# The low part of k laid out twice, so that both score products use 128 rows

## Chip, cores and metric

The kernel runs on one core of one Trainium2 chip. The metric is the device time of one execution, in microseconds (us); the time before is 1805.77 us, the median of three runs (1802.51 to 1806.38). PE is the matrix engine, PEld its weight loads, DVE VectorE, ACT ScalarE, POOL GpSimd, SP the engine that issues most transfers.

## The reference

Two layers of a transformer trunk over 256 latent tokens and 256 context tokens of width 1024. In each layer three attention branches and a Fourier branch read one projection; their gated sum is projected out and normalised, and an expert-choice layer of 16 experts follows. In the second layer only the latent tokens go on. The attention has four query heads of 64 features and two key heads, each shared by two query heads:

```python
def gqa_softmax(q, k, v, bias=None, sink=None):
    s = jnp.einsum("bqhgd,bkhd->bhgqk", q, k).astype(jnp.float32) * HEAD_DIM ** -0.5
    if bias is not None:
        s = s + bias
    ...
        p = jax.nn.softmax(s, axis=-1)
    return jnp.einsum("bhgqk,bkhd->bqhgd", p.astype(v.dtype), v)
```

The branches differ in what stands around it: branch a normalises and rotates q and k, branch c has a window and a sink, branch d a bias by relative position.

## The kernel before

Everything is float32, but the wide products run on operands of type fp32r, which the kernel splits itself: a value is hi + lo, and a product is taken as hi by hi, hi by lo and lo by hi. In the scores the split lies along the contraction. A head has 64 features, so a column of q holds 128 rows, hi above lo (lo above hi for the second key head). The tile of q, `qT`, has a block of 128 tokens' columns for each query head. The tile of k, `kT`, has three blocks of 512 tokens: hi over hi for each of the two key heads, and one block with the lo of key head 0 in rows 0 to 63 and that of key head 1 in rows 64 to 127. Two products make a score: `qT` by the hi block on all 128 rows, which gives hi by hi and lo by hi (line 642), and hi of q by lo of k on the 64 rows where both lie (line 643).

`post_vec` makes the parts in token order for one tile of 128 tokens (the copy of hi twice on ACT, line 595; lo on DVE, line 597), `post_tr` transposes them on PE (q in line 615, k in line 619) and moves them out of the bank with ACT (line 616) and with DVE (the cast of line 620). `scores` then makes the scores of one unit: either 128 latent tokens and one key head with 512 columns for two heads, or 128 context tokens with 256 columns for four heads. The scores lie in one tile of two banks, `ps`; DVE takes the maximum (line 676), ACT the exponential (line 681). One unit later the probabilities are transposed (lines 702 and 712), and after that multiplied by v (lines 724 and 733). Layer 0 has 18 units (three branches, four latent and two context each), layer 1 has 12.

This work isn't a stage of its own. `post_fill` and `attn_fill` put pieces of it into a queue, and the loops over the projection (line 531) and over the gates of the previous branches take a piece for each of their steps. A step of the gates has 24 products of line 771 and six of line 782, with weights that ACT and DVE split (lines 422 and 424) after a transfer; most steps have a modulation product too (line 217). On PE, the products of the gates and of the projection keep their order among themselves; the attention's pieces are placed between them, on PE, DVE and ACT, by a scheduler when the program is built. The order of SP's transfers and of POOL's work is that of the program text. Behind the attention come the output projection, the routing, and the experts, whose weights (1 MB a piece) go in turn into every large tile that the rest leaves free, the tile of k among them.

Two pools matter for the change: the tile of k is the only one with its tag `k8`, and the parts `o` share the tag `p` with the probabilities, whose tile is 128 by 1024.

Of the kernel before, what the change touches and what calls it, by code (L numbers as in the profile page):

```python
# [9 lines left out]
F32 = mybir.dt.float32  # L10
F32R = mybir.dt.float32r
# [75 lines left out]
def trunk(ctx: ExitStack, tc: tile.TileContext, x, c, ctx_in, c_ctx, w_mod, b_mod, w_in, qk_gain,  # L87
# [52 lines left out]
    def load_consts(l):  # L140
        """The mixers' tables, which give their place to weights once a layer's attention is done."""
        mix_cst.append(big([128, N_MIX], "cst"))
        nc.sync.dma_start(mix_cst[-1], consts[:, 0:N_MIX])
        if l == 0:
            nc.sync.dma_start(route_cst, consts[:, N_MIX:N_CONST])
# [10 lines left out]
    def ones():  # L156
        # the last column of the triangle
        return const("tri")[:, 127:128].to_broadcast([128, 128])
# [51 lines left out]
    def mod_mm(l, ch, group):  # L210
        """Partial products of one chunk, in rows 2q and 2q + 1 of each quadrant (q the chunk's place in its four)."""
        q = ch % 4
        p = ps_t()
        for r in range(2):
            for g in range(4):
                kt = 4 * r + g
                T.matmul(p[g * 32:g * 32 + 32, :], c_st[:, kt, 6 - 2 * q:38 - 2 * q], RAW["mod", l, ch, r][:, g, :],  # L217
                         start=r == 0, stop=r == 1)
        if ch == group[0]:
            mrows[l, group] = t2([128, 512])  # L220
            V.tensor_copy(mrows[l, group], p)
        else:
            m = mrows[l, group]
            V.tensor_tensor(m, m, p, op=OP.add)

    def mod_acc(l, ch, group):
        """As mod_mm, but the chunks of a group add up in a bank of their own."""
# [15 lines left out]
    def mod_tr(l, group):  # L243
        """Sums of up to four chunks, feature-major."""
# [14 lines left out]
    def mod_first(kp):  # L259
        """Shift and scale of two feature tiles, the first layer's."""  # L260
# [32 lines left out]
    def affine(l, half):  # L293
        """u = z * A + B, feature-major: the modulation, with the norm's own gain and bias folded in."""
# [64 lines left out]
    def ex_raw(l, e, kind, q):  # L359
        w = {"g": w_gate, "u": w_up, "d": w_down}[kind]  # L360

        if e == NE - 1 and kind == "d":
            # the last expert's share of the output comes by columns
            def go(t):
                nc.sync.dma_start(t, w[l, e, :, q * 256:q * 256 + 256].rearrange("(k p) n -> p k n", p=128))
            return (("ex", l, e, kind, q), [128, 8, 256], go)
# [12 lines left out]
    def ex_w(l, e, kind, k, c, n):  # L379
        """Rows k * 128.. and columns c..c + n of an expert's matrix."""  # L380
# [24 lines left out]
    def inorder(*engines):  # L405
        """What the block puts on these engines issues after the previous such block's work."""
# [10 lines left out]
    def split(key, src, alloc, eng=V):  # L417
        """hi + lo parts, each exact in the product's 12-bit significand."""
# [37 lines left out]
    def layer(l):  # L456
# [7 lines left out]
        def ut_alloc():  # L464
            if last:
                # a tile per stream: the context's go after the projections
# [33 lines left out]
        def bias_table():  # L500
            """Per-row relative-position bias, 8x, flipped into token order."""
# [43 lines left out]
        def post_alloc(m):  # L545
            qk[m] = (big([128, 4, 512], "q8", F32R), big([128, 3, 512], "k8", F32R))
            vv[m] = pool.tile([128, 4, 128], F32, name="v", tag="v", bufs=1)

        def rope(src, t, nh):
            """Rotates src [128, nh, 64] in place."""  # L550
# [11 lines left out]
        def post_norm(m, t):  # L562
            """Values aside; the norm's factors."""
# [15 lines left out]
        def post_vec(m, t):  # L579
            """norm and rotation of one token tile, split."""  # L580
# [9 lines left out]
            if lat and m != "d":  # L590
                rope(src, t, nh)
            o = b4([128, 14, 64], "p", F32R)
            ok, oq = o[:, 0:6], None
            kv_ = src[:, nq:nh]
            A.activation(ok[:, 0:4].rearrange("p (k u) d -> p k u d", u=2),
                         kv_.unsqueeze(2).to_broadcast([128, 2, 2, 64]), AF.Copy)
            V.tensor_tensor(ok[:, 4:6], kv_, ok[:, 0:4].rearrange("p (k u) d -> p k u d", u=2)[:, :, 0].bitcast(F32),
                            op=OP.subtract)
            if nq:
                oq = o[:, 6:14].rearrange("p (h s) d -> p h s d", s=2)  # L600
# [6 lines left out]
        def post_tr(m, t):  # L607
            """q blocks [hi | lo] ([lo | hi] for the second kv head), k blocks [hi | hi] x 2, [lo0 | lo1]."""
# [8 lines left out]
            p = ps_t([128, 3, 128])  # L617
            for b in range(3):
                T.transpose(p[:, b], ok[:, 2 * b:2 * b + 2].rearrange("p s d -> p (s d)").bitcast(F32), ident)
            V.tensor_copy(kT[:, :, ts], p)  # L620

# [6 lines left out]
        def br_out(m, src, kv, ts):  # L628
            """src [128, kv, tokens] to the branch, split."""
# [4 lines left out]
        def scores(m, u):  # L634
# [3 lines left out]
            def qk_mm(dst, h, t, k0, k1):  # L638
                kv = h // 2
                r = slice(64 * kv, 64 * kv + 64)  # L640
                ts = slice(t * 128, t * 128 + 128)
                T.matmul(dst, qT[:, h, ts], kT[:, kv, k0:k1], start=True, stop=False)  # L642
                T.matmul(dst, qT[r, h, ts], kT[r, 2, k0:k1], start=False, stop=True)  # L643
# [181 lines left out]
        def residual(dst, z, key):  # L825
            """alpha times the norm's output, from its normalised rows."""
# [6 lines left out]
        def y0_mm(kt):  # L833
            """Left half of the output: one merged feature tile's share, all tokens."""
# [45 lines left out]
        NS = NT // 2  # L880

        def route_weights():
            """The norm and the modulation folded into the router: logits = rstd * (h.wA - mean * sum(wA)) + B.w"""
# [15 lines left out]
        def turned(t, hf):  # L899
            """Half of the features of a token tile, feature-major."""  # L900
# [7 lines left out]
        def route_half(t, hf):  # L908
            """Router products of one half of the features of a token tile."""
# [4 lines left out]
            for k in range(4):  # L914
                # rows 0..15 of a quadrant sum its share; rows 16..31 are not used
# [20 lines left out]
        def route(t):  # L936
            """Router probabilities of one token tile; its rows normalised."""
# [14 lines left out]
        def rows(t):  # L952
            """Normalises a token tile."""
# [6 lines left out]
        def choose():  # L960
            """Slot number (1..CAP, 0 for none) of each token with each expert of its stream."""
# [34 lines left out]
        def gather(gr, s, pr):  # L996
            """Rows of the tokens that two experts chose, turned feature-major and modulated."""
# [25 lines left out]
        def gather_one(s, e):  # L1023
            """As gather, for one expert of the first group."""
# [21 lines left out]
        def scat_mat(gr):  # L1046
# [7 lines left out]
            else:  # L1054
                # the rows bring their weights along: a matrix of ones
# [96 lines left out]
        def scat_hl(s, dh):  # L1152
            """The last group's without its last expert, split."""
# [13 lines left out]
        # The last expert: partial sums over the features in row blocks (c, stream, slot), columns a quarter at  # L1167
        # a time, scattered by a matrix of ones that adds the parts up.
# [26 lines left out]
        def scat_start(t):  # L1195
            """The latents' banks begin with the rows so far."""
# [65 lines left out]
        def end_stats(s):  # L1262
            """Of both token tiles of a stream."""
# [37 lines left out]
        # ================= order of work =================  # L1301
# [379 lines left out]
    # emission: loads run LEAD tiles ahead of their use  # L1681
# [67 lines left out]
```

## Time and profile before

| | us |
|---|---|
| median of three runs | 1805.77 |
| lowest, highest | 1802.51, 1806.38 |
| span of the profiled execution | 1799.7 |
| PE busy in it | 1575.4 (88%) |
| DVE busy | 694.8 (39%) |
| ACT busy | 432.3 (24%) |

The profile is of one execution; the span runs from its first instruction to its last, and what lies around it isn't in it, so it is shorter than the runs' times. Its own time as a run would measure it isn't listed, so the span stands beside the median. Busy shares are means over the whole span. PE's durations are modelled at their ends and overlap, so a step of PE is read as the time from one instruction's start to the next one's.

### The profile page before, as it was taken

The numbers are of one execution on the slowest core, as the hardware profiler recorded it, in microseconds if no ns is written. First come the engines' busy times: TensorE is split into PE (matmuls) and PEld (weight loads), VectorE is DVE, ScalarE is ACT, GpSimd is POOL, SyncE is SP. The second block draws the span as 40 slices with busy tenths as digits, with TensorE's granted clock in tenths as the row PEclk, the third lists the DMA queues.
The fourth block names the chain that finished last, engine by engine and source line by source line (L and its number), as shares of the span: only waits on it lengthen the run. The fifth ranks groups of instructions, "written<-read, shape, count | busy, mean of one in ns | idle before, by whom it ended". The sixth has DMA issues, their size and how long they took to land.

```text
span 1799.7 us, 22915 instructions
## 1 busy us (share of the span) xinstructions
PE 1575.4 (88%) x9291; PEld 892.1 (50%) x9291; DVE 694.8 (39%) x1378; ACT 432.3 (24%) x929; POOL 129.7 (7%) x176
## 2 busy tenths in 40 slices
PE   7999999999989989899998899999978666667666
PEld 4767777768864333323332578888832211112112
DVE  3454453554452332222222585747543111102114
ACT  2343433343231110201200354544321001001000
POOL 1200112111110000000000320111100000000000
PEclk9999999999989999999999999999989889888888
DMA  9444344444559999999999664646889999999996
GB/s 310 164 149 157 119 167 107 164 140 165 216 208 365 374 408 409 409 409 409 409 409 403 234 240 169 216 111 236 327 317 409 409 409 409 409 409 409 409 409 245
DMA packets 194120, 533.04 MB, mean 296 GB/s; under 512 B 9520, under 2 KB 61088, under 8 KB 194016
## 3 DMA queue, kind: packets, MB, share of 16 engines
q1 hardware_dynamic: 192016, 527.49, 76.9%
q0 software_dynamic: 1856, 4.02, 1.3%
q8 instruction: 73, 1.20, 0.3%
q14 instruction: 31, 0.25, 0.0%
q10 hardware_dynamic: 144, 0.07, 0.0%
HBM read 530.50 MB, written 1.05 MB: 295 GB/s over the span
## 4 chain that ended last, share of the span: by engine, by line
PE 67%; DMA 15%; issue 10%; DVE 5%; ACT 2%; POOL 1%; SPq 0%; ACTq 0%; DVEq 0%; POOLq 0%
PE mm L771 14%; PE mm L1088 12%; PE mm L531 7%; DMA w<-in_w_up_dram 6%; PE mm L1109 5%; DMA raw<-in_w_up_dram 4%; PE mm L782 3%; PE pt L217 2%; PE mm L1122 2%; PE mm L851 2%; PE ps L1005 2%; DMA w<-in_w_down_dram 2%; PE ps L643 2%; PE pt L724 1%; PE ps L642 1%
## 5 line engine op out<-in xcount | busy, mean ns | idle before, releaser
L771 PE MATMUL mm<-w,b 128*128 128x512 f32 (+1 forms) x1536 | 292.6, 342 | 0.3 <-DVE b L424 0.3
L771 PEld LDWEIGHTS mm<-w,b 128*128 128x128 f32 x1536 | 236.8, 189 | 47.7 <-issue 18.6
L1077 ACT ACTIVATE t<-mm 128x512 f32<-128x512 f32 (+1 forms) x32 | 19.0, 594 | 663.2 <-PE mm L1122 352.1
L1078 DVE SCALAR_TENSOR_TENSOR t<-t,mm 128x512 f32<-128x512 f32 (+1 forms) x32 | 21.9, 684 | 358.6 <-ACT t L1077 358.5
L424 DVE TENSOR_TENSOR b<-raw,b 128x1024 fp32r<-128x1024 f32 (+1 forms) x95 | 112.7, 1189 | 122.7 <-ACT b L422 119.7
L531 PE MATMUL mm<-b,w 128*128 128x512 f32 (+1 forms) x720 | 148.9, 360 | 5.2 <-ACT b L422 3.6
L531 PEld LDWEIGHTS mm<-b,w 128*128 128x128 f32 x720 | 115.9, 192 | 30.7 <-ACT b L422 4.0
L422 ACT ACTIVATE b<-raw 128x1024 fp32r<-128x1024 f32 (+1 forms) x96 | 97.9, 1021 | 128.9 <-PE mm L771 97.5
L1095 DVE TENSOR_TENSOR k<-mm,b 32x512 f32<-32x512 f32 (+1 forms) x96 | 53.1, 553 | 187.5 <-PE mm L1109 84.6
L1088 PE MATMUL mm<-w,b 128*64 128x512 f32 x480 | 116.9, 596 | 2.1 <-DMA w<-in_w_gate_dram 1.2
L1122 PE MATMUL mm<-w,b 128*32 128x512 f32 x416 | 82.5, 665 | 26.9 <-DMA w<-in_w_up_dram 22.3
L800 POOL TENSOR_TENSOR b<-b,t 128x256 f32<-128x256 f32 x72 | 56.4, 798 | 521.6 <-DVE t L794 502.4
L1122 PE MATMUL mm<-raw,b 128*32 128x512 f32 x256 | 55.4, 733 | 30.8 <-DMA raw<-in_w_up_dram 16.1
L782 PE MATMUL mm<-w,wbs 128*128 128x512 f32 (+1 forms) x384 | 78.4, 339 | 0.1
L1088 PEld LDWEIGHTS mm<-w,b 128*64 128x64 f32 x480 | 37.9, 137 | 70.3 <-issue 63.9
L1088 PE MATMUL mm<-raw,b 128*64 128x512 f32 x280 | 70.9, 594 | 0.7 <-DMA raw<-in_w_gate_dram 0.7
L782 PEld LDWEIGHTS mm<-w,wbs 128*128 128x128 f32 x384 | 61.2, 188 | 8.8 <-ACT w L631 0.3
L1109 PE MATMUL mm<-w,t 128*64 128x512 f32 x240 | 58.4, 612 | 2.9 <-ACT t L1104 2.9
L1122 PEld LDWEIGHTS mm<-w,b 128*32 128x32 f32 x416 | 16.3, 116 | 86.8 <-DMA w<-in_w_up_dram 41.4
L681 ACT ACTIVATE p<-ps,st 128x512 f32<-128x512 f32 (+1 forms) x72 | 43.6, 613 | 55.3 <-DVE st L679 55.3
L1146 PE MATMUL ps<-k,wbs 128*128 128x512 f32 x72 | 39.7, 671 | 4.7 <-DVE k L1095 3.7
L1122 PEld LDWEIGHTS mm<-raw,b 128*32 128x32 f32 x256 | 9.8, 118 | 65.8 <-DMA raw<-in_w_up_dram 28.7
(373 smaller groups left out, 2232.6 us busy)
## 6 DMA issues: line engine op xcount, KB each, us to landing
w<-in_w_up_dram SPq DMA_DIRECT2D x64, 1024.0 KB, 18.1
w<-in_w_down_dram SPq DMA_DIRECT2D x59, 1024.0 KB, 16.6
raw<-in_w_mod_dram SPq DMA_DIRECT2D x48, 1024.0 KB, 5.2
w<-in_w_gate_dram SPq DMA_DIRECT2D x48, 1024.0 KB, 18.3
raw<-in_w_in_dram SPq DMA_DIRECT2D x46, 1024.0 KB, 6.3
raw<-in_w_down_dram SPq DMA_DIRECT2D x35, 1024.0 KB, 16.1
raw<-in_w_up_dram SPq DMA_DIRECT2D x34, 1024.0 KB, 15.3
raw<-in_w_gate_dram SPq DMA_DIRECT2D x33, 1024.0 KB, 15.3
```

Of the source, the lines that this page charges most:

```text
L422: A.activation(hi, src, AF.Copy)
L424: eng.tensor_tensor(lo, src, hi.bitcast(F32), op=OP.subtract)
L531: T.matmul(p, uu(kt, t * 128, t * 128 + 128), ww[:, kt % 2, a:n], start=kt == 0 and i == 0, stop=kt == 7 and i == 2)
L681: A.activation(P[:, hh, a:b], s[:, hh, a:b], AF.Exp, scale=0.125, bias=nm[:, n:n + 1], accum_out=rs[:, n:n + 1])
L771: T.matmul(p, ww[:, kt], uu(kt, 0, NTOK), start=n == 0, stop=n == 23)
L782: T.matmul(p, ww[:, k, o:o + 128], br[i][:, j, k], start=n == 0, stop=n == 5)
L800: G.tensor_tensor(m, m, e[:, c], op=OP.add)
L1088: T.matmul(p[fh * 64:fh * 64 + 64], xs[kt // 4][:, kt % 4, e % 4], ex_w(l, e, kind, kt, fh * 512, 512), start=kt == 0, stop=kt == 7)
L1095: V.tensor_tensor(dst, pd[q], g, op=OP.mult)
L1109: T.matmul(pd[dh * 64:dh * 64 + 64], hT[:, q, fh * 64:fh * 64 + 64], ex_w(l, e, "d", f, dh * 512, 512), start=f == 0, stop=f == 7)
L1122: T.matmul(p[r:r + 32], xs[kt // 4][:, kt % 4, e % 4], ex_w(l, e, kind, kt, fh * 512, 512), start=kt == 0, stop=kt == 7)
L1146: T.matmul(p[:, dh], loc["sm", gr][:, s, t], loc["y", gr][s][:, dh * 512:dh * 512 + 512], start=True, stop=True)
```

## The change

The tile of k gets four blocks in place of three: hi over hi for both key heads, then lo over lo for both. The second product so reads the whole column of q, 128 rows, and adds hi by lo and also lo by lo. In the diff the lines that only lose a comment are left out.

```diff
-            qk[m] = (big([128, 4, 512], "q8", F32R), big([128, 3, 512], "k8", F32R))
+            qk[m] = (big([128, 4, 512], "q8", F32R), big([128, 4, 512], "k8", F32R))
...
-            o = b4([128, 14, 64], "p", F32R)
-            ok, oq = o[:, 0:6], None
+            o = b4([128, 16, 64], "p", F32R)
+            ok, oq = o[:, 0:8].rearrange("p (i k u) d -> p i k u d", i=2, u=2), None
             kv_ = src[:, nq:nh]
-            A.activation(ok[:, 0:4].rearrange("p (k u) d -> p k u d", u=2),
-                         kv_.unsqueeze(2).to_broadcast([128, 2, 2, 64]), AF.Copy)
-            V.tensor_tensor(ok[:, 4:6], kv_, ok[:, 0:4].rearrange("p (k u) d -> p k u d", u=2)[:, :, 0].bitcast(F32),
-                            op=OP.subtract)
+            kv2 = kv_.unsqueeze(2).to_broadcast([128, 2, 2, 64])
+            A.activation(ok[:, 0], kv2, AF.Copy)
+            V.tensor_tensor(ok[:, 1], kv2, ok[:, 0].bitcast(F32), op=OP.subtract)
             if nq:
-                oq = o[:, 6:14].rearrange("p (h s) d -> p h s d", s=2)
+                oq = o[:, 8:16].rearrange("p (h s) d -> p h s d", s=2)
...
-            p = ps_t([128, 3, 128])
-            for b in range(3):
-                T.transpose(p[:, b], ok[:, 2 * b:2 * b + 2].rearrange("p s d -> p (s d)").bitcast(F32), ident)
+            p = ps_t([128, 4, 128])
+            for b in range(4):
+                T.transpose(p[:, b], ok[:, b // 2, b % 2].rearrange("p s d -> p (s d)").bitcast(F32), ident)
             V.tensor_copy(kT[:, :, ts], p)
...
-                r = slice(64 * kv, 64 * kv + 64)
                 ts = slice(t * 128, t * 128 + 128)
-                T.matmul(dst, qT[:, h, ts], kT[:, kv, k0:k1], start=True, stop=False)
-                T.matmul(dst, qT[r, h, ts], kT[r, 2, k0:k1], start=False, stop=True)
+                for i in range(2):
+                    T.matmul(dst, qT[:, h, ts], kT[:, 2 * i + kv, k0:k1], start=i == 0, stop=i == 1)
```

The change also moves instructions, since the scheduler places the attention's pieces anew. On SP and POOL nothing moves. On PE, at the first scores of layer 0's first branch (the row names the line, the tile written and those read, and the output's shape; in the kernel after the change, lines from 599 on are numbered one lower, from 644 on two lower, the copy on ACT is line 596, and both score products stand in line 641), the order before is:

```order
L615 MATMUL pt<-idsel,p 128x128 x4
L619 MATMUL pt<-idsel,p 128x128 x3
L771 MATMUL mm<-w_146,b_854 128x512
L771 MATMUL mm<-w_146,b_855 128x512
L217 MATMUL pt<-raw,c_st 32x512
L642 MATMUL ps<-k_688,q_687 128x512
L643 MATMUL ps<-k_688,q_687 128x512
L642 MATMUL ps<-k_688,q_687 128x512
L643 MATMUL ps<-k_688,q_687 128x512
L217 MATMUL pt<-raw,c_st 32x512 x7
```

and after the change:

```order
L614 MATMUL pt<-idsel,p 128x128 x4
L618 MATMUL pt<-idsel,p 128x128 x4
L769 MATMUL mm<-w_146,b_857 128x512
L217 MATMUL pt<-raw,c_st 32x512
L641 MATMUL ps<-k_688,q_687 128x512 x4
L217 MATMUL pt<-raw,c_st 32x512 x7
L769 MATMUL mm<-w_146,b_858 128x512
```

The second row has a fourth transpose, one product of the gates has moved from ahead of line 217 to behind it, and the four score products are of one form.

At the first context unit of the same branch, with the probabilities' transposes ahead and the products with v between, PE has before:

```order
L702 MATMUL pt<-idsel,p 128x128 x8
L642 MATMUL ps<-k_688,q_687 128x256
L643 MATMUL ps<-k_688,q_687 128x256
L642 MATMUL ps<-k_688,q_687 128x256
L643 MATMUL ps<-k_688,q_687 128x256
L642 MATMUL ps<-k_688,q_687 128x256
L724 MATMUL pt<-pt,v 64x128 x8
L643 MATMUL ps<-k_688,q_687 128x256
L642 MATMUL ps<-k_688,q_687 128x256
L643 MATMUL ps<-k_688,q_687 128x256
L217 MATMUL pt<-raw,c_st 32x512 x8
```

and after:

```order
L700 MATMUL pt<-idsel,p 128x128 x8
L641 MATMUL ps<-k_688,q_687 128x256 x5
L722 MATMUL pt<-pt,v 64x128 x8
L641 MATMUL ps<-k_688,q_687 128x256 x3
L217 MATMUL pt<-raw,c_st 32x512 x8
```

Here nothing changes its place; the eight score products stand in the same two parts, five and three, around line 724.

## Rows read from the trace of the kernel before

**Rows 1.** The page, the chain that ended last: shares of the span by engine.

```profile
PE 67%; DMA 15%; issue 10%; DVE 5%; ACT 2%; POOL 1%; SPq 0%; ACTq 0%; DVEq 0%; POOLq 0%
```

**Rows 2.** Busy time by stage: us, then each engine, clock, DMA share, GB/s.

```profile
110.00:385.00 275.00, 273.96 (x1470) 199.34 (x1469) 138.05 (x273) 101.63 (x231) 29.09 (x41) 1.00 0.41 134
...
1060.00:1240.00 180.00, 179.34 (x1313) 148.22 (x1311) 117.88 (x222) 83.69 (x181) 18.54 (x24) 1.00 0.55 175
...
1375.00:1799.00 424.00, 281.33 (x1976) 84.62 (x1976) 77.83 (x152) 28.15 (x68) 5.51 (x7) 0.86 0.99 392
```

**Rows 3.** PE's timeline, a token unit's scores: start us, us, engine, line, instruction.

```profile
118.72 1.55 PE L782 MATMUL mm<-w,wbs 128*128 128x512 f32 x6
120.11 1.04 PE L702 MATMUL pt<-idsel,p 128*128 128x128 f32 x8
120.90 0.47 PE L642 MATMUL ps<-k,q 128*128 128x512 f32 x1
121.31 0.50 PE L643 MATMUL ps<-k,q 64*128 64x512 f32 x1
...
122.16 0.50 PE L643 MATMUL ps<-k,q 64*128 64x512 f32 x1
122.59 1.65 PE L771 MATMUL mm<-w,b 128*128 128x512 f32 x6
```

**Rows 4.** PE's timeline, a context unit's scores of 256 columns.

```profile
153.20 0.36 PE L642 MATMUL ps<-k,q 128*128 128x256 f32 x1
...
154.74 1.09 PE L724 MATMUL pt<-pt,v 128*64 128x128 f32 x16
```

**Rows 5.** The chain in order of time, line 771 at 512 and 256 columns.

```profile
122.66 5.67 PE mm L771 x24
...
1254.88 2.87 PE mm L771 x24
```

**Rows 6.** PE's timeline, late scores of layer 0's third branch.

```profile
359.02 0.40 PE L642 MATMUL ps<-k,q 128*128 128x512 f32 x1
359.35 0.49 PE L643 MATMUL ps<-k,q 64*128 64x512 f32 x1
359.77 0.50 PE L642 MATMUL ps<-k,q 128*128 128x512 f32 x1
360.11 1.03 PE L702 MATMUL pt<-idsel,p 128*128 128x128 f32 x8
```

**Rows 7.** Groups by line and shape: count, busy us, mean ns, idle before, releasers.

```profile
L642 PEld LDWEIGHTS ps<-k,q 128*128 128x128 f32 x72 | 13.5, 187 | 12.7 <-issue 5.8 <-DVE k L620 3.4 <-ACT p L681 0.9
L643 PEld LDWEIGHTS ps<-k,q 64*128 64x128 f32 x72 | 13.2, 183 | 15.1 <-issue 13.1
...
L620 DVE CAST k<-pt 128x384 fp32r<-128x384 f32 x24 | 13.1, 553 | 5.7 <-PE pt L619 5.6
...
L597 DVE TENSOR_TENSOR p<-t,p 128x128 fp32r<-128x128 f32 x24 | 7.3, 303 | 1.6 <-ACT p L595 1.6
```

**Rows 8.** Timeline of all engines from the first scores on.

```profile
108.71 0.56 DVE L620 CAST k<-pt 128x384 fp32r<-128x384 f32 x1
...
109.08 1.04 PE L217 MATMUL pt<-raw,c_st 128*32 128x512 f32 x2
...
110.05 0.49 PE L642 MATMUL ps<-k,q 128*128 128x512 f32 x1
...
113.73 0.69 DVE L224 TENSOR_TENSOR t<-t,pt 128x512 f32<-128x512 f32 x1 [0.64 <-PE pt L217]
...
119.17 1.23 DVE L424 TENSOR_TENSOR b<-raw,b 128x1024 fp32r<-128x1024 f32 x1 [2.00 <-ACT b L422]
```

**Rows 9.** Busy time between layer 0's attention and its experts.

```profile
440.00:460.00 20.00, 20.00 (x89) 16.34 (x88) 8.37 (x13) 6.33 (x11) 2.86 (x4) 1.00 0.16 53
...
480.00:500.00 20.00, 20.00 (x123) 16.19 (x122) 11.47 (x23) 4.01 (x10) 0.60 (x1) 1.00 0.97 377
```

**Rows 10.** The chain in order of time, its first long transfer in layer 1.

```profile
1374.19 18.98 DMA raw<-in_w_up_dram
```

## The prediction

> **What bounds the kernel now.** I read the page first: the chain of work that ended last is 67% PE and 15% DMA [rows 1]. That is an average over unlike stages, so next came the busy time by stage. The score products stand in layer 0's attention (110 to 385 us) and layer 1's (1060 to 1240 us). There PE is busy 273.96 of 275 and 179.34 of 180 us at a granted clock of 1.00, while the DMA engines are 0.41 and 0.55 busy; the last 424 us are the reverse, DMA 0.99 and PE 281 us [rows 2]. So what PE saves in the attention counts, if the expert stage behind it starts earlier by as much.
>
> Then PE's timeline around one unit of scores. The six products of line 782 (128 rows, 512 columns) take from 118.72 to 120.11, 0.232 us each. The four score products, alternately 128 and 64 rows, start at 120.90 and the next instruction at 122.59: 0.423 us each for the same columns [rows 3]. For a context unit's 256 columns, five products take from 153.20 to 154.74, 0.308 each [rows 4]; 24 products of line 771 take 2.87 us with 256 columns and 5.67 us with 512, 0.120 and 0.236 each [rows 5]. Both widths lose 0.19 us a product, so the loss isn't streaming.
>
> Where it sits shows at 359 us: line 642 behind a product of its own form, with line 643 next, takes 0.33 us; line 643 between two of the other form 0.42; line 642 behind line 643, with 128-row transposes next, 0.34 [rows 6]. So a neighbour of another form costs some 0.1 us on each side, **0.19 us for each change of form**. The weight loads say the same: line 643's have 13.1 us of idle time ahead of them that nothing released, line 642's 5.8 [rows 7].
>
> **The change, part by part.**
>
> *The second score product on 128 rows.* Line 643 runs 72 times, so there are 144 places where 64 rows meet something else. The order of instructions keeps 18 of them as changes after the edit, since the neighbour there is itself of another form: line 217 (128*32) or line 724 (128*64) follows in 12, line 724 precedes in 6, as in the context unit shown above. 126 changes go: 82 in layer 0, 44 in layer 1. At 0.19 us that is 126 x 0.19 = **23.9 us off PE**. Bounds: 0.185 (0.308 - 0.120, rounded down) gives 23.3, and 0.20 (the two half costs of 0.10) 25.2. The number of score products, their columns and the weight loads' columns stay, and the loads take 183 ns with 64 rows and 187 ns with 128 [rows 7].
>
> A page of the Trainium skill puts a figure on the undisturbed step: TensorE: Matmul & The Clock Gate, Back-to-back issue gap, gives about 131 ns for a stream of weight loads and products at 512 columns. The trace disagrees with 232 ns. By the page's figure the 96 wide products would save an estimated 96 x 0.10 = 10 us more; the measured step decides.
>
> *One transpose more for each token tile.* 24 tiles (four token tiles, three branches, two layers) get a fourth transpose. Eight of them (line 702) fill 0.79 us up to line 642's start, 0.10 each, and 1.04 to their own end, 0.13 [rows 3]. I take 0.11: 24 x 0.11 = **2.6 us onto PE**, between 2.4 and 3.1.
>
> *VectorE.* The subtraction of line 597 goes from 128 to 256 columns and the cast of line 620 from 384 to 512. The cast takes 553 ns, the subtraction 303 ns [rows 7], and a 512-column instruction that reads a bank (line 224) 0.69 us [rows 8]. So the cast grows by 0.14, and the subtraction, a third of the way from 128 to 512 columns, by 0.13: 24 x 0.27 = 6.5 us. VectorE is busy 138 of 275 and 118 of 180 us there [rows 2], so I cost it at nothing beside PE's products of line 771, except at the place where the scores need the cast; without that cover it is the whole 6.5 us. ScalarE's copy keeps its size.
>
> *The first scores of a branch.* Line 642's loads have 3.4 us of idle time ahead of them in four places that the profile puts down to the cast of the last k tile [rows 7]. In the first of them the cast ends at 108.71 + 0.56 = 109.27, but line 642 starts at 110.05, when line 217's two products, begun at 109.08, are through [rows 8]. So most of that wait is line 217's, and the cast has up to 0.8 us in hand. After the edit the cast is 0.14 longer, and in layer 0 the order has one product of line 771 fewer (0.23) ahead of the scores; that product isn't lost, it comes later. Line 217 fills in for it in two of the three branches. If no cover were left, the wait would grow by 4 x 0.37 = 1.5 us; at least it is 0. I take **0.2 us**, near the lower end, since the row shows the cover. Queued behind these scores on PE are the rest of line 217 and the next gate products, so it is PE time.
>
> *What else could give it back.* With PE faster by 0.8 us in such a unit, the gate weights must keep up. VectorE's split for the next products (line 424) ends at 119.17 + 1.23 = 120.40 [rows 8] and the products that read it start at 122.59 [rows 3]: 2.2 us of slack against 0.8. The wait for the score banks (line 681 before line 642) is 0.9 us in four places [rows 7]; that chain runs from one score product's end to the next, so it moves along with them. No allocation grows: the k tile takes the place of a 128x2x1024 weight tile, and the p tile of 16 x 64 is as large as the probabilities that share its tag. No order of transfers changes.
>
> *Does it reach the end?* Behind the attention the DMA share is 0.16 at 440 to 460 us and 0.97 at 480 to 500 [rows 9]: the expert weights don't stream until PE's work frees their tiles. So the stream starts earlier by what the attention saves. In layer 1 the first long transfer on the chain that ended last comes at 1374.19 [rows 10], behind a start that the attention sets. I pass the saving through whole.
>
> *Sum*: 23.9 - 2.6 - 0.2 = **21.1 us**. The profiled span, 1799.7 us, becomes 1778.6; the median of the runs shown, 1805.77, lies 6.1 us above that span, which I keep: 1784.7 us. With all ends against it, 23.3 - 3.1 - 6.5 - 1.5 = 12.2 (1793.6); with all ends for it, 25.2 - 2.4 = 22.8 (1783.0).
>
> **The rivals.**
>
> *Half of it passes.* By the 82 and 44 changes, layer 0 saves 15.6 - 1.3 - 0.1 = 14.2 and layer 1 8.4 - 1.3 - 0.1 = 7.0 us. If the expert stage of layer 0 ends when its weights have come (16 experts of three 4 MB matrices), whatever the start, only layer 1's share is left, 1798.8; if layer 1's softmax chain eats its share (VectorE is busiest there, 118 of 180 us [rows 2]), 14.2 are left, 1791.6. Against both speaks that transfers wait for tiles, and that the four waits for the score banks sum to 0.9 us.
>
> *It is hidden.* If transfers bounded the whole span, nothing would show: 1805.8. Against it speaks the DMA share of 0.41 and 0.55 in the attention [rows 2].
>
> *Slower.* The loss might not lie in the rows but in two products that add into one bank with weights loaded between. Then the 128-row form pays the same 0.42 us, and transposes and wait come on top: 2.6 + 1.5 = 4.1 us, 1809.9; with VectorE's 6.5 as well, 1816.4. It decides if a 128-row second product still starts 0.42 us after the first. Line 771 speaks against it: it also adds into one bank with other weights each time, at 0.236 [rows 5]; so does line 642's 0.33 where only one neighbour differs [rows 6]. The Trainium skill has a rule on that side: TensorE: Matmul & The Clock Gate, in the part on what happens when a matmul is issued, says that a weight load's time goes by its columns and that the row count doesn't matter. The loads' durations agree with it; the starts of the products around them don't, which is why I leave this rival little.
>
> **How the numbers follow.** Three runs of the kernel before lie within 1802.51 to 1806.38, so 0.2% (3.6 us) is about what can be told from no change. The forecast, 1784.7, gets 0.80; one layer's share alone 0.11; hidden 0.05; slower 0.04. The forecast's own bounds, 1783 to 1794, widened by 4 us below (the runs' scatter, and a cost of a change that I may have too low) and by 1 us above, where the one-layer case of 1791.6 already lies inside, give 1779 to 1795. Faster by over 0.2%: 0.80 + 0.11 + a little of the hidden case, 0.92; within: 0.05; slower: 0.03.
>
> **What would show it.** Score products at 0.23 us a step within a unit and 0.12 for 256 columns, with no idle time ahead of the second's weight load; a unit of four some 0.8 us shorter; both attention stretches shorter by about 14.2 and 7.0 us; the expert stages as long as before. It is wrong if the step stays at 0.42, if the waits for the cast grow past 1.5 us, or if the stretch from 385 to 1060 us grows by what the attention saved.

## The result and the profile after

The kernel after takes 1785.74 us, the median of four runs (1783.75 to 1788.05), against 1805.42 us for the kernel before (four runs, 1802.51 to 1806.38). The ratio is 0.9895, with a 95% interval of 0.9882 to 0.9908: faster by 19.7 us, where 21.1 were forecast and 1784.7 us named. The profiled execution spans 1783.9 us and took 1786.01 as a run measures it, so 2.1 us lie around the span.

The page after, its busy times by engine and the chain that ended last, answers to [rows 1]:

```profile
PE 1556.6 (87%) x9315; PEld 891.8 (50%) x9315; DVE 700.0 (39%) x1378; ACT 432.7 (24%) x929; POOL 131.6 (7%) x176
...
PE 66%; DMA 15%; issue 11%; DVE 5%; ACT 2%; POOL 1%; SPq 0%; ACTq 0%; DVEq 0%; POOLq 0%
```

PE is 18.8 us less busy (1575.4 before) and VectorE 5.2 us more (694.8); the chain's shares are the same within a per cent. The means over the span so hardly show a change that gave 19.7 us; the stages do. Busy time by stage after, the two attentions and the last 423 us, with the columns of [rows 2]:

```profile
110.00:371.00 261.00, 258.61 (x1451) 196.49 (x1451) 137.69 (x268) 99.60 (x222) 28.71 (x41) 1.00 0.44 142
1050.00:1225.00 175.00, 174.49 (x1332) 150.43 (x1330) 120.34 (x223) 83.91 (x181) 20.88 (x24) 1.00 0.57 180
1355.00:1778.00 423.00, 283.19 (x1984) 85.47 (x1980) 78.59 (x153) 28.56 (x69) 5.51 (x7) 0.87 1.00 395
```

PE still fills both attentions at a granted clock of 1.00, and the DMA engines have room there (0.44 and 0.57); the last stage is bound by transfers as before, and begins earlier.

PE's timeline after: the same three kinds of places as [rows 3, 4, 6].

```profile
120.23 1.03 PE L700 MATMUL pt<-idsel,p 128*128 128x128 f32 x8
121.02 1.17 PE L641 MATMUL ps<-k,q 128*128 128x512 f32 x4
122.02 3.36 PE L769 MATMUL mm<-w,b 128*128 128x512 f32 x14
...
152.16 0.83 PE L641 MATMUL ps<-k,q 128*128 128x256 f32 x5
152.92 1.09 PE L722 MATMUL pt<-pt,v 128*64 128x128 f32 x16
...
345.02 1.17 PE L641 MATMUL ps<-k,q 128*128 128x512 f32 x4
346.03 4.95 PE L769 MATMUL mm<-w,b 128*128 128x512 f32 x21
```

Four score products go from 121.02 to 122.02, 0.25 us each, where [rows 3] has 1.69 us for four. The first takes 0.31 us behind the transposes, the other three 0.22 to 0.24 each. Five of 256 columns take 0.76 us, 0.152 each, the last one's step ahead of line 722's other form included, where [rows 4] has 0.308 each. The transposes ahead of them take 0.79 us as before.

Groups by line and shape after, for [rows 7]:

```profile
L641 PEld LDWEIGHTS ps<-k,q 128*128 128x128 f32 x144 | 22.8, 188 | 8.1 <-DVE k L619 2.5 <-issue 2.0 <-ACT p L679 1.4
L619 DVE CAST k<-pt 128x512 fp32r<-128x512 f32 x24 | 16.4, 685 | 5.9 <-PE pt L618 5.6
...
L597 DVE TENSOR_TENSOR p<-t,p 128x256 fp32r<-128x256 f32 x24 | 10.3, 427 | 1.6 <-ACT p L596 1.6
```

The idle time that nothing released, 13.1 + 5.8 us before, is 2.0. The cast and the subtraction grew by 132 and 124 ns (forecast: 140 and 130). The scores' wait for the cast didn't grow: 2.5 us, from 3.4.

### The profile page after: what moved, and what is told of

Read it like the earlier page. It is cut to its first block, busy times and chain, and to the rows that moved or that the text cites. A ratio compares the mean times of both kernels' runs of the same rounds, so it can differ in the third digit from the quotient of the medians.

```text
span 1783.9 us, 22960 instructions
## 1 busy us (share of the span) xinstructions
PE 1556.6 (87%) x9315; PEld 891.8 (50%) x9315; DVE 700.0 (39%) x1378; ACT 432.7 (24%) x929; POOL 131.6 (7%) x176
## 4 chain that ended last, share of the span: by engine, by line
PE 66%; DMA 15%; issue 11%; DVE 5%; ACT 2%; POOL 1%; SPq 0%; ACTq 0%; DVEq 0%; POOLq 0%
PE mm L769 14%; PE mm L1086 12%; PE mm L531 7%; DMA w<-in_w_up_dram 6%; PE mm L1107 5%; DMA raw<-in_w_up_dram 4%; PE mm L780 3%; PE mm L1120 2%; PE pt L217 2%; PE mm L849 2%; DMA w<-in_w_down_dram 2%; PE ps L1003 2%; PE ps L641 2%; PE pt L722 1%; PE ps L1144 1%
## 5 line engine op out<-in xcount | busy, mean ns | idle before, releaser
L1120 PE MATMUL mm<-w,b 128*32 128x512 f32 x416 | 92.3, 725 | 30.5 <-DMA w<-in_w_up_dram 25.6
L1120 PE MATMUL mm<-raw,b 128*32 128x512 f32 x256 | 49.2, 664 | 31.1 <-DMA raw<-in_w_up_dram 17.4
L1086 PEld LDWEIGHTS mm<-raw,b 128*64 128x64 f32 x280 | 22.0, 137 | 40.8 <-issue 38.9
```

The source lines that it names most:

```text
L1086: T.matmul(p[fh * 64:fh * 64 + 64], xs[kt // 4][:, kt % 4, e % 4], ex_w(l, e, kind, kt, fh * 512, 512), start=kt == 0, stop=kt == 7)
L1120: T.matmul(p[r:r + 32], xs[kt // 4][:, kt % 4, e % 4], ex_w(l, e, kind, kt, fh * 512, 512), start=kt == 0, stop=kt == 7)
```

## The experiments

Four kernels ran on one chip (before: 1803.5 us there). The first question is whether the loss lies in the rows, and what one change of form costs.

**The products grouped by form.** The 64 rows stay, but a unit makes its 128-row products of two heads first and then their 64-row ones, which leaves 403 of the 463 changes of form that PE's whole trace shows before.

```diff
...
-                for hh in range(2):
-                    qk_mm(s[:, hh], 2 * kv + hh, t, 0, 512)
+                for part in range(2):
+                    for hh in range(2):
+                        qk_mm(part, s[:, hh], 2 * kv + hh, t, 0, 512)
...
-                for kv in range(2):
-                    for hh in range(2):
-                        qk_mm(s[:, kv, hh * 256:hh * 256 + 256], 2 * kv + hh, t, 256, 512)
+                for hh in range(2):
+                    for part in range(2):
+                        for kv in range(2):
+                            qk_mm(part, s[:, kv, hh * 256:hh * 256 + 256], 2 * kv + hh, t, 256, 512)
```

> The kernel before with the same 144 score products, half of them still on 64 rows, but in another order: in a unit first the 128-row products of two heads, then their 64-row products. The order of instructions on PE has 95 changes of form at the scores in place of 155, and no transpose, cast or column more. Theory (each change of form costs 0.19 us): 60 x 0.19 = 11.4 us faster, 1794.0 us; 64-row products that stand behind one another take 0.33 us or less with 512 columns. Rival (a 64-row product is slow in itself, wherever it stands): no change, 1805.4 us, and steps of 0.42 us stay.

Measured: 1790.29 us, ratio 0.993 (0.9917 to 0.9942), 13.2 us less by the medians, for 60 changes. PE's timeline of this kernel, a latent unit and a context unit:

```profile
121.07 0.70 PE L643 MATMUL ps<-k,q 128*128 128x512 f32 x2
121.70 0.73 PE L645 MATMUL ps<-k,q 64*128 64x512 f32 x2
122.36 3.92 PE L775 MATMUL mm<-w,b 128*128 128x512 f32 x16
...
152.57 0.38 PE L645 MATMUL ps<-k,q 64*128 64x256 f32 x2
152.88 0.38 PE L643 MATMUL ps<-k,q 128*128 128x256 f32 x1
```

The latent unit takes 1.29 us for four products, between the 1.69 before and the 1.00 after: the same products and rows, two changes in place of four. So a good part of the loss lies in the neighbours, not in the products. The context unit shows something else: its two 64-row products together take 0.31 us, as long as one did in [rows 4]. They read different halves of the rows (k head 0 and k head 1) and run side by side. In the two stretches of the table below this kernel is 12.8 us shorter.

**The layout alone.** The kernel after, but the second product reads 64 rows of the new blocks.

```diff
-                for i in range(2):
-                    T.matmul(dst, qT[:, h, ts], kT[:, 2 * i + kv, k0:k1], start=i == 0, stop=i == 1)
+                r = slice(64 * kv, 64 * kv + 64)
+                T.matmul(dst, qT[:, h, ts], kT[:, kv, k0:k1], start=True, stop=False)
+                T.matmul(dst, qT[r, h, ts], kT[r, 2 + kv, k0:k1], start=False, stop=True)
```

> The change without its second product: four k blocks, four transposes, the longer subtraction and cast, but line 643's product still on 64 rows. Theory: 24 transposes at 0.11 us and 0 to 2 us of waits, 2.6 to 4.6 us slower than before, 1808.0 to 1810.0 us. Rival (VectorE's 6.5 us are not hidden): 1814.5 us or more. Rival (the gain came from where the scheduler put things anew, which this kernel shares in part): faster than before.

Measured: 1807.5 us, ratio 1.0028 (1.0017 to 1.0039), 4.0 us more by the medians, 3 to 7 by the interval. PE's timeline, the same unit:

```profile
122.65 0.47 PE L641 MATMUL ps<-k,q 128*128 128x512 f32 x1
123.05 0.50 PE L642 MATMUL ps<-k,q 64*128 64x512 f32 x1
...
124.34 1.88 PE L770 MATMUL mm<-w,b 128*128 128x512 f32 x7
```

The unit is back at 1.69 us. The new layout by itself gains nothing, so the gain isn't that of new places either, and it costs more than the 2.8 us that the prediction's two terms make. The profiled execution, at 1811.49 us, is the slowest of this kernel's seven.

**The rows alone.** The kernel before, with its three blocks and transposes; the second product reads all 128 rows of the third block, which adds q's lo by the other key head's lo, a term that isn't in the reference.

```diff
...
-                T.matmul(dst, qT[r, h, ts], kT[r, 2, k0:k1], start=False, stop=True)
+                T.matmul(dst, qT[:, h, ts], kT[:, 2, k0:k1], start=False, stop=True)
```

> The kernel before with its three k blocks, three transposes and shorter VectorE work, but the second product reads all 128 rows of the third block. That adds the product of q's low part with the other key head's low part, so the scores differ slightly from the reference's. Theory: 126 changes of form go and nothing is added, 23.9 us faster than before, 1781.5 us, and some 3 to 5 us faster than the changed kernel (transposes 2.6, waits up to 2). Rival (two products into one bank cost 0.42 us whatever their rows): 1805.4 us.

Measured: 1780.16 us, ratio 0.9879 (0.9864 to 0.9894), 23.3 us less by the medians. PE's timeline:

```profile
121.47 0.47 PE L641 MATMUL ps<-k,q 128*128 128x512 f32 x1
121.78 0.39 PE L642 MATMUL ps<-k,q 128*128 128x512 f32 x1
122.01 0.39 PE L641 MATMUL ps<-k,q 128*128 128x512 f32 x1
122.24 0.40 PE L642 MATMUL ps<-k,q 128*128 128x512 f32 x1
122.47 3.81 PE L770 MATMUL mm<-w,b 128*128 128x512 f32 x16
```

The two products of a score still add into one bank with other weights each time, and the second follows the first by 0.31 us behind the transposes and by 0.23 after that. (The 0.08 us more isn't a loss: the step of the last transpose ahead is as much shorter, 0.03 us where the others take 0.11. This is so in all the kernels, and some 0.02 us of each of the 0.423 in the prediction is this.) The rival of the shared bank needed 0.42.

**The kernel before once more**, to have a second profiled execution of it.

> The kernel before, unchanged, for a second profile and the scatter. The profiled span of before was 1799.7 us, that of the changed kernel 1783.9 us, 15.8 us apart, while the medians are 19.7 us apart. If the profiled execution of before was a quick one, this span lies near 1803 us (the median less the 2.1 us that the changed kernel's runs have outside their spans). If the spans are typical, it lies near 1799.7 us again and the medians' difference is scatter.

Measured: 1803.57 us, ratio 0.9999 (0.999 to 1.0007). Its profiled execution spans 1801.7 us and took 1803.53, 1.8 us around the span; the one of [rows 1 to 10] spans 1799.7, so it was a quick one.

The next three ran on another chip (before: 1803.87 us) and ask what the layout's own cost is: PE's transposes, VectorE, or something else.

**Two transposes of k.** hi and lo of both key heads are transposed once each, and four copies of half the partitions lay them twice, two on ACT and two on DVE.

```diff
...
-            for b in range(4):
-                T.transpose(p[:, b], ok[:, b // 2, b % 2].rearrange("p s d -> p (s d)").bitcast(F32), ident)
-            V.tensor_copy(kT[:, :, ts], p)
+            for i in range(2):
+                T.transpose(p[:, i], ok[:, i].rearrange("p k d -> p (k d)").bitcast(F32), ident)
+            for kv in range(2):
+                src = p[64 * kv:64 * kv + 64]
+                A.activation(kT[0:64, kv::2, ts], src, AF.Copy)
+                V.tensor_copy(kT[64:128, kv::2, ts], src)
```

> The changed kernel with two transposes of k in place of four: hi of both key heads in one, lo of both in the other, and the doubling done when the bank is emptied, by two copies of 64 partitions and 256 columns on VectorE and two on ScalarE in place of one cast of 512 columns. In token order the copy and the subtraction shrink to 128 columns. Theory: 48 transposes at 0.11 us go from PE, 5.3 us, and one or two of them come back as waits for the copies, 3 to 5 us faster than the changed kernel (which is 0.9895 of before): ratio to before 0.987 to 0.988. Rival (ScalarE's two copies for each tile delay what is queued behind them, as the gate weights): same as the changed kernel or slower, 0.9895 to 0.992.

Measured: 1782.63 us, ratio 0.9885 (0.987 to 0.9899), 2.0 us below the kernel after on the same chip (1784.66, told below), with intervals that overlap; the theory's 3 to 5 us didn't come. The steps of k's transposes sum to 3.9 us in place of 9.3, so most of these 5.4 us went elsewhere. Groups by line of this kernel, the copies:

```profile
L622 DVE CAST k<-pt 64x256 fp32r<-64x256 f32 x48 | 20.1, 423 | 12.1 <-ACT k L621 11.1
L621 ACT ACTIVATE k<-pt 64x256 fp32r<-64x256 f32 x48 | 18.0, 376 | 12.6 <-DVE k L622 10.3 <-PE pt L618 1.8
```

Each engine waits for the other's copy, so four copies come one after another, about 1.6 us (2 x 423 + 2 x 376 ns) where one cast took 0.69. PE then pays in other lines: 1.4 us more in the scores' steps and 2.2 us more in those of the gates' products.

**The subtraction of lo made twice**, the same work once more on VectorE, to price that engine.

```diff
             V.tensor_tensor(ok[:, 1], kv2, ok[:, 0].bitcast(F32), op=OP.subtract)
+            V.tensor_tensor(ok[:, 1], kv2, ok[:, 0].bitcast(F32), op=OP.subtract)
```

> The changed kernel with the subtraction of line 597 done twice: 24 x 0.43 = 10.3 us more of VectorE, nothing else. Theory (VectorE's part of the change is hidden but for small waits): within 1.5 us of the changed kernel, ratio to before 0.9895 to 0.9903. Rival (VectorE's work in the attention is on the path, and so took the 2 us by which the change fell short in its stretches): 0.995.

Measured: 1781.76 us, ratio 0.988 (0.9866 to 0.9895). Groups by line of this kernel:

```profile
L598 DVE TENSOR_TENSOR p<-t,p 128x256 fp32r<-128x256 f32 x24 | 10.8, 451 | 0.1
...
L217 PE MATMUL pt<-raw,c_st 128*32 128x512 f32 x288 | 38.8, 599 | 0.1
```

and PE's timeline in layer 1:

```profile
1122.67 0.41 PE L615 MATMUL pt<-idsel,p 128*128 128x128 f32 x2 [0.57 <-DVE p L604]
```

10.8 us more of VectorE's time didn't make it slower than the kernel after (1784.66); it came out 2.9 us lower, with intervals that overlap. VectorE's work is hidden but for a small part: in layer 1 PE waits 1.0 us for VectorE's part of q, where the kernel after waits 0.4. The test isn't clean, since the scheduler placed the longer work otherwise, and line 217 is 38.8 us busy where the kernel after has 39.8. The two stretches of the table below come out 0.3 us shorter in sum, with 1.0 us less of line 217's steps in them, so at most some 1 us of the 10.8 shows. Line 217 gave the next lead.

**The kernel after once more.**

> The changed kernel, unchanged, on the chip of the other two and with more rounds: ratio to before 0.9895, interval some 0.002 wide. Its stretch of gate products in layer 0 383.4 us and in layer 1 224.9 us, as in its first profile, within 0.5 us; if the wait of 0.8 us near 143 us in layer 0 came from one late transfer, it is not there again and layer 0's stretch is 382.6.

Measured: 1784.66 us, ratio 0.9898 (0.9881 to 0.9914), span 1782.4. Layer 0's stretch is 382.1 us and layer 1's 224.8, and the wait near 143 us isn't there again. What line 217's block looks like in the kernel after, PE's timeline of its first profile in layer 1:

```profile
1127.65 0.38 PE L618 MATMUL pt<-idsel,p 128*128 128x128 f32 x2
1127.97 1.05 PE L217 MATMUL pt<-raw,c_st 128*32 128x512 f32 x2
1128.94 0.44 PE L618 MATMUL pt<-idsel,p 128*128 128x128 f32 x2
1129.31 1.92 PE L217 MATMUL pt<-raw,c_st 128*32 128x512 f32 x14
1131.16 1.09 PE L769 MATMUL mm<-w,b 128*128 128x256 f32 x7
```

and in the kernel before:

```profile
1141.02 1.92 PE L217 MATMUL pt<-raw,c_st 128*32 128x512 f32 x16
1142.88 0.86 PE L771 MATMUL mm<-w,b 128*128 128x256 f32 x5
```

A block is eight products (128 rows, 32 columns of weights), and the trace has two records for each. The first product's two stand between k's transposes and take 0.97 us there, while the other fourteen records take 1.85 behind it. In the kernel before this block isn't split, and all sixteen take 1.86.

**Two transposes, all four copies on VectorE**, so that the engines don't wait for each other. The edit is against the kernel of two transposes.

```diff
...
-                A.activation(kT[0:64, kv::2, ts], src, AF.Copy)
+                V.tensor_copy(kT[0:64, kv::2, ts], src)
                 V.tensor_copy(kT[64:128, kv::2, ts], src)
```

> The kernel of two transposes with all four copies on VectorE. In its profile with two on ScalarE the two engines wait for each other at these copies, 10.3 and 11.1 us, and PE gets 1.6 us in its two stretches out of the 5.6 us that the transposes free. Theory (it is these waits that give the rest back): VectorE's copies need no other engine and have cover, as the doubled subtraction showed, so 2 to 3 us more than with ScalarE; but the order on PE has 4 changes of form more than the changed kernel, 0.2 to 0.5 us each. Ratio to before 0.987 to 0.988, layer 0's stretch near 380.5 us, layer 1's near 223.5 us. Rival (the first scores wait for four copies of 0.42 us): stretches as in the changed kernel, 382.1 and 224.8 us, ratio 0.9898.

Measured: 1785.12 us (before on this chip: 1804.6), ratio 0.9904 (0.9888 to 0.992): no gain left over the kernel after. Layer 0's stretch is 381.1 us, 1.0 shorter, but layer 1's is 226.6, where 223.5 was expected and the kernel after has 224.8. The new order there costs more than the copies give: 1.9 us more in the steps of line 217, which is split at two places more, and 2.3 more in those of the six products of each gate step (line 783 here), where PE waits up to 0.8 us for VectorE's part of q. Groups by line of this kernel:

```profile
L217 PE MATMUL pt<-raw,c_st 128*32 128x512 f32 x288 | 41.9, 599 | 0.7 <-PE mm L772 0.6
```

The last two ask whether such splits cost what they seem to (before: 1805.54 us).

**Line 217's blocks kept whole.** In the kernel after, each block of line 217 is placed behind the latest transposes or scores of the attention on PE, by an order edge when the program is built; 329 changes of form stay of the 339 in PE's trace.

```diff
...
+    @contextmanager
+    def attn_pe():
+        start = len(nc.cur_bb.bb.instructions)
+        yield
+        for i in nc.cur_bb.bb.instructions[start:]:
+            if i.engine == mybir.EngineType.PE:
+                attn_tail[0] = i
...
-                ev(lambda: mod_mm(ll, ch, g), mod_raw(ll, ch))
+                def behind():
+                    with ExitStack() as es:
+                        if attn_tail[0] is not None:
+                            es.enter_context(tc.issue_after(attn_tail[0]))
+                        mod_mm(ll, ch, g)
+                ev(behind, mod_raw(ll, ch))
```

> The changed kernel with line 217's modulation products (128*32) bound to issue behind the last score products and transposes of k that stand ahead of them in the program, so that the eight of a block are no longer split. In the changed kernel five blocks are split, four around the first scores of a branch and one around transposes in layer 1; the order on PE has 10 changes of form fewer here. Theory: a change of form costs whatever the forms are, and a split of line 217, whose products are long, about 0.97 us, as its sum of steps in layer 1 (13.06 us against 12.09 without the one split): 5 x 0.97 = 4.9 us, less the waits for the cast that the first part of the block covered, 0 to 0.8 us in four places: 1.7 to 4.9 us faster than the changed kernel, ratio to before 0.987 to 0.989. Rival (line 217 only filled PE's wait for the cast): as the changed kernel, 0.9898.

Measured: 1778.35 us, ratio 0.9855 (0.9836 to 0.9874), 27.2 us below the kernel before. Groups by line of this kernel:

```profile
L217 PE MATMUL pt<-raw,c_st 128*32 128x512 f32 x288 | 34.6, 598 | 0.0
...
L651 PEld LDWEIGHTS ps<-k,q 128*128 128x128 f32 x144 | 22.9, 188 | 5.6 <-ACT p L689 1.4 <-issue 1.0 <-DVE k L629 0.9
```

Line 217 is 5.2 us less busy for five splits fewer; by its steps 4.85 us, 0.97 a split. The two stretches are 5.1 us shorter in sum than in the kernel after once more, a little more than the theory's upper end, and the ratio lies below the expected 0.987 to 0.989. The line's products were no needed cover for the first scores: their wait for the cast is 0.9 us without them, 2.5 with.

**Whole blocks and two transposes** together, that edit and the one with copies on both engines.

> Both edits on the changed kernel: line 217 unsplit, and two transposes of k with two copies on VectorE and two on ScalarE. Theory: the two gains of the stretches add, 1.7 us (of the two transposes) and 1.7 to 4.9 us: ratio to before 0.986 to 0.988. Rival (the copies come later than the cast and line 217 no longer covers that wait): no better than the unsplit kernel alone.

Measured: 1777.81 us, ratio 0.9853 (0.9838 to 0.9869). It is the lowest of all, and its two stretches are 1.2 us shorter than those of the one before it, but the two intervals don't tell them apart, so it isn't shown that the gains add. Both beat both kernels.

Where the time lies, by the start of PE's instructions (us): layer 0 from the first product of the gates (line 771 before, 769 after) to its last, then to the first of layer 1, layer 1 likewise, and from its last to the end of the span.

| | layer 0 | between | layer 1 | to the end |
|---|---|---|---|---|
| before [rows 1 to 10] | 395.32 | 580.76 | 230.80 | 511.66 |
| before once more | 395.54 | 581.71 | 230.88 | 511.48 |
| rows alone | 380.62 | 581.72 | 222.82 | 510.27 |
| grouped by form | 387.54 | 582.07 | 226.07 | 511.04 |
| layout alone | 397.31 | 583.51 | 234.65 | 511.73 |
| after | 383.42 | 581.87 | 224.87 | 512.62 |
| after once more | 382.13 | 580.99 | 224.84 | 512.39 |
| two transposes | 381.26 | 581.67 | 224.09 | 511.62 |
| subtraction twice | 382.45 | 579.25 | 224.20 | 511.83 |
| copies on VectorE | 381.11 | 581.23 | 226.60 | 512.06 |
| line 217 whole | 379.21 | 582.99 | 222.67 | 512.06 |
| whole, two transposes | 378.37 | 580.88 | 222.30 | 512.20 |

The boundary rows, PE's timeline of the kernel before once more (the second and last row are the last 24 products of a layer, whose last starts 5.21 and 2.75 us later):

```profile
82.05 1.05 PE L771 MATMUL mm<-w,b 128*128 128x512 f32 x3
...
472.38 5.61 PE L771 MATMUL mm<-w,b 128*128 128x512 f32 x24
...
1059.31 0.47 PE L771 MATMUL mm<-w,b 128*128 128x256 f32 x1
...
1287.44 3.03 PE L771 MATMUL mm<-w,b 128*128 128x256 f32 x24
```

and of the kernel after once more:

```profile
82.05 1.05 PE L769 MATMUL mm<-w,b 128*128 128x512 f32 x3
...
458.97 5.61 PE L769 MATMUL mm<-w,b 128*128 128x512 f32 x24
...
1045.17 0.47 PE L769 MATMUL mm<-w,b 128*128 128x256 f32 x1
...
1267.26 3.03 PE L769 MATMUL mm<-w,b 128*128 128x256 f32 x24
```

Layer 0 ends 13.41 us earlier (472.38 - 458.97) and layer 1 is 6.04 us shorter ((1287.44 - 1059.31) - (1267.26 - 1045.17)). These two are the executions that are compared below.

## Why the prediction was right

**The cause.** The loss goes with the change of form between neighbours. The rows alone, on the old layout, give 23.3 us; the layout alone gives none; fewer changes with the same rows give a part. The slower rival (two products into one bank) falls with the 0.23 us step of the rows alone.

**126 changes at 0.19, 23.9 us.** From the kernel before once more to the rows alone, layer 0 loses 14.92 us and layer 1 8.06: 23.0, against 15.6 and 8.4. Over 82 and 44 changes that is 0.182 and 0.183 us each, just under the lower bound of 0.185. Of it, 21.2 us are steps of the score products (54.6 to 33.4); the other 1.8 lie in the steps of the neighbours, as [rows 6] had it. The Trainium skill, TensorEngine Tiling (Array Packing), Tiling Modes, Key Properties, says that changing the tiling mode drains the engine; the runs agree that a change costs, 0.18 us each, and don't show what in it takes the time.

**Layout: 2.6 us of transposes, 0.2 of waits, VectorE at nothing.** From the rows alone to the kernel after once more, layer 0 grows by 1.51 and layer 1 by 2.02 us: 3.5, where 2.8 were forecast. The transposes' steps took 2.73 of it (24 x 0.114): a fourth transpose's own step is 0.109, and 0.15 us stand beside the split that comes next. VectorE's term holds: doubling the subtraction, 10.8 us more, shows with some 1 us at most. The wait for the cast shrank in the view that puts it down (3.4 to 2.5), so 0.2 was not too little.

**The term that was missing** is one split of a block of line 217 in layer 1, 0.97 us (13.06 us for its 96 steps against 12.09 or 12.10 in kernels without it). With the transposes' 1.47 that makes 2.4 in layer 1, where the stretch grew by 2.0; the gates' steps are 0.4 shorter. I had the orders of both kernels, and counted the changes at the score products alone; over all of PE 124 go, not 126. Two changes at 0.18 would be 0.37 us; why the split costs more stands in the last section. Two runs in which this block stays whole agree with the price: with the subtraction made twice (12.09), and with all blocks whole, five splits at once.

**Layer by layer**, 13.4 and 6.0 us came, where 14.2 and 7.0 were forecast. Of the 1.6 us missing in sum (19.45 for 21.1), the price of a change took 0.9 and the layout 0.7: both lie on the same side, so the sum isn't right by terms that cancel. The first profile of the kernel after is 1.3 us longer in layer 0 than the second. PE's and ACT's timeline of that first profile:

```profile
141.77 1.06 ACT L422 ACTIVATE b<-raw 128x1024 fp32r<-128x1024 f32 x1 [1.72 <-DMA raw<-in_w_in_dram]
142.73 0.58 ACT L702 ACTIVATE pt<-pt 128x512 f32<-128x512 f32 x1
143.36 1.09 PE L722 MATMUL pt<-pt,v 128*64 128x128 f32 x16 [0.76 <-ACT pt L702]
```

One late transfer held ACT's split, behind it stood the move of the probabilities, and PE waited 0.76 us for it. The second profile runs 0.95 us later up to here; in it this split starts at 141.07 with no wait, 1.65 us sooner by that. The other 0.53 us are a longer wait of q's transposes for ACT at 212 us (1.36, then 0.83). It is a matter of one execution; the two medians differ by 1.1 us.

**Carried to the end.** "Between" and "to the end" stay within 579.2 to 583.5 and 510.3 to 512.6 us in the table, with no pattern that goes with the savings before them. So the half-passes and the hidden rival fall: both layers' savings arrive whole.

**The level.** The 6.1 us that I kept between span and median aren't what lies around a span: that is about 2 us (1786.01 for 1783.9; 1803.53 for 1801.7). The execution of [rows 1 to 10] was some 4 us shorter than the median run. To take the median as the level was right nonetheless; the span plus 2 would have given 1780.6.

**A difference that the clock made.** The layout alone adds 3.8 us to layer 1 where the kernel after adds 2.0 to the rows alone. The longer steps of k's transposes (1.47) and the split (0.96) are in both. What the layout alone has beyond that is TensorE's clock in its one profiled execution. Busy time by stage of this kernel, with the columns of [rows 2]:

```profile
1060.00:1064.00 4.00, 1.76 (x7) 1.01 (x7) 3.41 (x8) 3.52 (x7) 1.20 (x1) 1.00 0.00 0
1064.00:1068.00 4.00, 4.00 (x18) 3.62 (x19) 3.42 (x6) 2.25 (x4) 0.00 (x0) 0.57 0.29 64
1068.00:1072.00 4.00, 4.00 (x37) 4.00 (x36) 3.09 (x9) 2.02 (x4) 0.00 (x0) 1.00 0.58 202
```

After a stretch in which PE was busy 1.76 of 4 us, the granted clock is 0.57 in the mean, most of it at the lower level (0.5, 1.2 GHz), and a product of 256 columns steps 0.21 us there in place of 0.12. The first 18 products of layer 1's stretch take 5.00 us, and 3.40 in the kernel after once more: 1.6 us, which leave 2.2 of the 3.8. The other runs wait there as well, and none has the lower clock within its two stretches, so why it fell in this one isn't shown.

**What stays open.** It isn't shown what within a change of form takes the 0.18 us.

## What to carry to other kernels

Count the neighbours whose rows or columns of the array differ, over the whole order and not only at the edited line: each change costs PE some 0.18 us, more than three quarters of a 512-column product here, so a product on fewer rows between full ones is dearer than the full one, even where half of that adds next to nothing. Where 64 rows must stay, group them, and put two that read different halves next to each other. And after a change that wins, look at what the scheduler split elsewhere: that was worth some 5 us here, a quarter of the gain, and lay mostly in products that no longer ran side by side.

## What the runs showed of the hardware

Two 64-row products on different halves of the rows start 3 to 4 ns apart in the grouped kernel's context units, while two on the same half (its latent units) start 0.335 us apart. The Trainium skill, TensorE: Matmul & The Clock Gate, in its part on packing small matmuls, says that products in distinct row groups run concurrently and start some 4 ns apart; the trace agrees. This accounts for what the kernel grouped by form gained beyond 60 changes at 0.19, which make 11.4 us: its twelve such pairs save one 256-column step of 0.12 each, 1.4 us, together 12.8, as in its two stretches (13.2 by the medians).

A block of line 217 that is broken pays 0.97 us, and the starts of its records show where. Its eight products of 32 columns write the four quarters of the bank's partitions in turn. In a whole block the sixteen records start in four groups of four, 5 to 8 ns apart within a group and 0.43 to 0.45 us from group to group. Broken after the first product, its two records start alone, 0.45 us apart, and the fourteen that are left still make four groups (4, 4, 3 and 3 records). So six groups stand where four were, in all five breaks of the kernel after, whether two, four or ten records stand ahead of the break: the price is two groups that run with fewer products side by side, and the two changes of form are a small part of it. By this count a break after the fourth product would add no group; no run has one.
